# A two-layer streaming encoder in fp32r: a combined first transfer, tokens of both halves scaled together, and weight-stationary pooling and convolution projections in the second layer

## The chip, the cores and the metric

The kernel runs on one core of a Trainium2 chip. The metric is the device time of one execution in microseconds; a profiled execution gives the span of the instructions and, beside it, its own device time.

## The reference

Two layers, each with a mixing part and a feed-forward part, on 256 tokens of 1024 channels:

```
h = rmsnorm(x, g_pre_mix)
c_q, c_kv, k_r, p_in, s_u, s_v, cv_b, cv_c, cv_x, gate_logits = split(h @ w_in)
y_a = mla_branch(c_q, c_kv, k_r, ...) @ w_br_a       # attention, 8 heads, low rank q and kv, rotary part
y_b = pool_branch(p_in, pool_w, pool_scale) @ w_br_b # trailing means over 2, 4, 8, 16 tokens
y_c = sgu_branch(s_u, s_v, ...) @ w_br_c             # gating over blocks of 128 tokens
y_d = conv_branch(cv_b, cv_c, cv_x, conv_w) @ w_br_d # z = cv_c * cv_x; y = cv_b * conv3(z)
x = x + rmsnorm((sum of sigmoid(gate_i) * y_i) @ w_out, g_post_mix)
h = rmsnorm(x, g_pre_ffn)
x = x + rmsnorm((silu(h @ w_ffn_gate) * (h @ w_ffn_up)) @ w_ffn_down, g_post_ffn)
```

All arrays are fp32.

## The kernel before, in words

**Products.** TensorE multiplies in fp32r. Each fp32 operand is split into a high part (rounded to fp32r) and a remainder, and a product is three matmuls (`mac`, L316 to L320): high by high, remainder of the tokens by high weights, high tokens by remainder of the weights.

**Tokens.** The 256 tokens are two halves h of 128. The normed input is kept transposed, channels on partitions: tiles `hh` and `hl` (high and remainder) per half, eight blocks of 128 channels each. The reciprocal root of the mean square is not applied to them; it scales the results of the projections, as a column per token (`rstd`).

**Weights.** All weights lie in DRAM as 268 pieces of up to 128 x 1024 (`wall`), in the order in which they are used (`piece_plan`). Each is loaded by SP into one of four landing buffers `st` (L253), converted by ScalarE to its high part (L268), and VectorE subtracts to get the remainder (L288); both go to buffers `u4` (u in the profile), of which there are 24. `pump` does this for one piece, `tick` calls it as long as fewer than about six converted pieces are unused, and `W` hands a piece out. A buffer comes back when its last matmul has read it.

**Order.** The order on each engine is the order of the calls: the kernel turns automatic scheduling off. Side work (attention, the small branches) stands in Python generators; `tick` is called after every unit of six matmuls and advances each generator whose delay has run out. The table at the top (PA, Y1, AS and others) sets these delays in ticks.

**The start.** ScalarE issues the DMAs of the first token block and of the table of constants `cst` (L367, L370); SP issues the first two weight pieces in halves, and more tokens. Fourteen rows of matmuls on zeros (NW = 7, L387) keep TensorE busy. Then tokens are scaled by the gains, a half at a time (`x_hi`, `x_lo`), and the first two pieces converted in halves (L581, L582). The first matmuls stand in L909.

**Second layer's projections.** Groups of columns of `w_in`: A (attention), S (spatial gating), P (pooling input and cv_b), C (cv_c and cv_x), then four gates of two 512-column blocks each. For P and C (L964, L966) tokens are stationary and the weights move: `group2` runs four pieces for two halves. ScalarE evicts a half with the scale `rstd` (L932, L936), VectorE multiplies cv_c by cv_x (L937). `g_misc` then transposes the results, 12 blocks of 128 x 128 on TensorE (L789, L793), into tiles with channels on partitions, in which pooling and convolution run along the free dimension.

**Feed-forward.** Here the kernel already has blocks with stationary weights (`block`, L1092): 128 columns of the weights are stationary and the tokens move, high and remainder parts of both halves side by side as 512 columns (L1097), then the weights' remainder by the 256 high columns (L1102). The result has channels on partitions; `total` (L1106) adds the two parts and multiplies by a row of scales `rrow`, made by two transposes (`g_rrow`).

Of the kernel before, what the change touches and what calls it, by code (L numbers as in the profile page):

```python
# [10 lines left out]
F32 = mybir.dt.float32  # L11
F32R = mybir.dt.float32r
# [29 lines left out]
PA, PB = 2, 4  # L42
SA, SB = 3, 3
NW = 7
# [28 lines left out]

def down_after(b):
# [37 lines left out]
def uses(key):  # L112

    if key[1] in ("wg", "wu"):
        return 1
    return 4 if key[1] in ("uq", "ukv") or key[1] == "fd" and key[2] >= NB - 4 else 2
# [80 lines left out]
def trunk(ctx: ExitStack, tc, x, xT, wall, small, const, qtab, gpost, out):  # L197
# [64 lines left out]

    def convert(i):
        key, w = PLAN[i]
        st = staged.pop(i)
# [88 lines left out]

    def hT_tiles(h):
        return T([P, NK, P], f"hh{h}", 1, F32R), T([P, NK, P], f"hl{h}", 1, F32R)
# [3 lines left out]
    cst = T([P, 96 + NL * SGW], "cst", 1, pool=cp)  # L360
# [195 lines left out]

    def x_hi(k, eng=nc.scalar):
        for h in range(2):
            o, i, g = ht[h][0][:, k, :], xt[k // 4][:, k % 4, h * P:(h + 1) * P], sg["gpm"][:, k:k + 1]
            if eng is nc.vector:  # L560
                nc.vector.tensor_scalar(o, i, g, None, op0=ALU.mult)
            else:
                nc.scalar.activation(o, i, AF.Identity, scale=g)

    def x_lo(k):
        for h in range(2):
            nc.vector.scalar_tensor_tensor(ht[h][1][:, k, :], xt[k // 4][:, k % 4, h * P:(h + 1) * P],
                                           sg["gpm"][:, k:k + 1], ht[h][0][:, k, :].bitcast(F32),
                                           op0=ALU.mult, op1=ALU.subtract)


    first_w = {i: (U([P, PIECE], F32R), U([P, PIECE], F32R)) for i in range(2)}
    state["free"] -= 4
    src = [staged.pop(i) for i in range(2)]
    for k in range(2):
        x_hi(k, nc.vector if k == 0 else nc.scalar)
        x_lo(k)
        for i in range(2):
            w = PLAN[i][1] // 2
            c = np.s_[:, k * w:k * w + w]  # L580
            nc.scalar.activation(first_w[i][0][c], src[i][c], AF.Copy)  # L581
            nc.vector.tensor_tensor(first_w[i][1][c], src[i][c], first_w[i][0].bitcast(F32)[c], op=ALU.subtract)  # L582
    for i in range(2):
        known(i, *first_w[i])
    state["cv"] = 2
    stage_to(5)
    for kp in range(1, 4):
# [22 lines left out]
    class Part:  # L610


        def __init__(self, tiles, s, h):
            self.tiles, self.s, self.h = tiles, s, h

        def __getitem__(self, at):
            k = at[1]
            return self.tiles[k // 2][:, k % 2, self.s, self.h * P:(self.h + 1) * P]
# [611 lines left out]
```

## Time and profile before

| | |
|---|---|
| Runs (3) | median 802.87 us, 802.28 to 803.49 |
| Profiled execution | 802.21 us |
| its span | 800.4 us |
| TensorE busy | 790.8 us (99%) |
| VectorE busy | 598.3 us (75%) |
| ScalarE busy | 452.6 us (57%) |
| DMA traffic | 148.11 MB, mean 185 GB/s |

Rows of the profile name an engine (PE is TensorE, PEld its weight loads, DVE VectorE, ACT ScalarE), a line of the kernel, an operation, the tile written and the tiles read, and how often; behind the bar or after the start stand durations. An arrow in brackets says what ended the idle time before an instruction. Matmuls overlap: a duration runs from issue to the last result, so the cost of one in a row of many is the distance between starts, which the chain of waits gives.

### The profile page before, as it was taken

The numbers are of one execution on the slowest core, as the hardware profiler recorded it, in microseconds if no ns is written. First come the engines' busy times: TensorE is split into PE (matmuls) and PEld (weight loads), VectorE is DVE, ScalarE is ACT, GpSimd is POOL, SyncE is SP. The second block draws the span as 40 slices with busy tenths as digits, with TensorE's granted clock in tenths as the row PEclk, the third lists the DMA queues.
The fourth block names the chain that finished last, engine by engine and source line by source line (L and its number), as shares of the span: only waits on it lengthen the run. The fifth ranks groups of instructions, "written<-read, shape, count | busy, mean of one in ns | idle before, by whom it ended". The sixth has DMA issues, their size and how long they took to land.

```text
span 800.4 us, 10903 instructions
## 1 busy us (share of the span) xinstructions
PE 790.8 (99%) x3982; PEld 666.3 (83%) x3982; DVE 598.3 (75%) x1094; ACT 452.6 (57%) x776; POOL 3.9 (0%) x16
## 2 busy tenths in 40 slices
PE   8999999999999999999999999999999999999996
PEld 8888887888888888888888888878888888888885
DVE  6687976758887777778895688764679787777773
ACT  7767655444665555455665675644367555455541
POOL 0000000000000000000000000000000000000000
PEclk9999999999999999999999999999999999999999
DMA  9866444465664565555655545455555555555631
GB/s 317 304 215 212 160 158 158 160 208 164 201 214 136 185 205 185 186 192 176 223 170 197 205 161 182 131 172 197 175 193 184 181 185 186 187 185 185 206 106 52
DMA packets 42245, 148.11 MB, mean 185 GB/s; under 512 B 4688, under 2 KB 5840, under 8 KB 42192
## 3 DMA queue, kind: packets, MB, share of 16 engines
q1 hardware_dynamic: 41328, 145.12, 54.4%
q0 software_dynamic: 576, 2.10, 0.8%
q8 instruction: 31, 0.51, 0.3%
q10 hardware_dynamic: 288, 0.21, 0.1%
q14 instruction: 22, 0.18, 0.1%
HBM read 146.36 MB, written 1.05 MB: 184 GB/s over the span
## 4 chain that ended last, share of the span: by engine, by line
PE 98%; DVE 1%; DMA 0%; ACT 0%; issue 0%; DVEq 0%; SPq 0%; ACTq 0%
PE acc L318 20%; PE acc L320 20%; PE acc L319 20%; PE mm L1097 17%; PE mm L1102 9%; PE tp L440 3%; PE mm L318 2%; PE mm L320 2%; PE mm L319 2%; PE mm L715 1%; PE acc L743 1%; PE acc L909 1%; DMA st<-wall 0%; PE mm L836 0%; PE mm L862 0%; DVE mrg L500 0%
## 5 line engine op out<-in xcount | busy, mean ns | idle before, releaser
L288 DVE TENSOR_TENSOR u<-st,u 128x1024 fp32r<-128x1024 f32 (+1 forms) x268 | 318.6, 1214 | 50.6 <-ACT u L268 50.0
L268 ACT ACTIVATE u<-st 128x1024 fp32r<-128x1024 f32 (+1 forms) x268 | 273.5, 1047 | 17.0 <-DMA st<-wall 16.8
L318 PE MATMUL acc<-u,hh 128*128 128x512 f32 (+1 forms) x424 | 169.1, 399 | 0.0
L320 PE MATMUL acc<-u,hh 128*128 128x512 f32 (+1 forms) x424 | 164.5, 388 | 0.0
L319 PE MATMUL acc<-u,hl 128*128 128x512 f32 (+1 forms) x424 | 164.2, 387 | 0.0
L1097 PE MATMUL mm<-u,u 128*128 128x512 f32 x576 | 144.4, 392 | 0.0
L1097 PEld LDWEIGHTS mm<-u,u 128*128 128x128 f32 x576 | 105.3, 188 | 20.8
L318 PE MATMUL acc<-u,s2k 128*128 128x512 f32 x256 | 101.2, 395 | 0.0
L320 PE MATMUL acc<-u,s2k 128*128 128x512 f32 x256 | 100.6, 393 | 0.0
L319 PE MATMUL acc<-u,s2k 128*128 128x512 f32 x256 | 100.3, 392 | 0.0
L320 PEld LDWEIGHTS acc<-u,hh 128*128 128x128 f32 x424 | 79.6, 188 | 16.2
L318 PEld LDWEIGHTS acc<-u,hh 128*128 128x128 f32 x424 | 79.7, 188 | 14.5 <-issue 0.3
L319 PEld LDWEIGHTS acc<-u,hl 128*128 128x128 f32 x424 | 79.8, 188 | 14.2
L1102 PEld LDWEIGHTS mm<-u,u 128*128 128x128 f32 x576 | 78.6, 190 | 5.6
L1102 PE MATMUL mm<-u,u 128*128 128x256 f32 x576 | 80.3, 282 | 0.0
L1025 ACT ACTIVATE gate<-acc,rhalf 128x512 f32<-128x512 f32 x32 | 22.0, 689 | 65.9 <-PE acc L320 65.7
L320 PEld LDWEIGHTS acc<-u,s2k 128*128 128x128 f32 x256 | 48.1, 188 | 10.1
L318 PEld LDWEIGHTS acc<-u,s2k 128*128 128x128 f32 x256 | 48.2, 188 | 9.3 <-issue 0.3
L319 PEld LDWEIGHTS acc<-u,s2k 128*128 128x128 f32 x256 | 48.1, 188 | 9.1
L1108 DVE TENSOR_TENSOR tok<-mm,tok 128x256 f32<-128x256 f32 x72 | 30.3, 420 | 27.7 <-ACT tok L1107 27.5
L1107 ACT COPY tok<-mm 128x256 f32<-128x256 f32 x72 | 26.6, 370 | 42.6 <-PE mm L1102 39.6
L443 ACT ACTIVATE s2k<-tok 128x256 fp32r<-128x256 f32 (+1 forms) x38 | 16.3, 429 | 53.8 <-DVE tok L1122 53.8
(172 smaller groups left out, 750.1 us busy)
## 6 DMA issues: line engine op xcount, KB each, us to landing
st<-wall SPq DMA_DIRECT2D x261, 512.0 KB, 3.8
st<-wall SPq DMA_DIRECT2D x7, 416.0 KB, 4.0
gpost<-gpost POOLq DMA_DIRECT2D x4, 512.0 KB, 4.7
x<-x SPq DMA_DIRECT2D x2, 512.0 KB, 6.0
small<-small SPq DMA_DIRECT2D x2, 512.0 KB, 4.2
u<-xT SPq DMA_DIRECT2D x3, 256.0 KB, 6.2
st<-wall SPq DMA_DIRECT2D x2, 256.0 KB, 4.3
out<-x SPq DMA_DIRECT2D x2, 256.0 KB, 2.0
```

Source lines behind the costliest of these rows:

```text
L268: nc.scalar.activation(hi[:, :w], st[:, :w], AF.Copy)
L288: nc.vector.tensor_tensor(lo[:, :w], st[:, :w], hi.bitcast(F32)[:, :w], op=ALU.subtract)
L318: nc.tensor.matmul(out_, a[0][aw], w[0][ws], start=start, stop=False)
L319: nc.tensor.matmul(out_, a[1][aw], w[0][ws], start=False, stop=False)
L320: nc.tensor.matmul(out_, a[0][aw], w[1][ws], start=False, stop=stop)
L440: nc.tensor.transpose(dst[:, i * P:(i + 1) * P], s, ident)
L443: nc.scalar.activation(hi, src, AF.Copy)
L1025: nc.scalar.activation(gt[h], pgt[h], AF.Tanh, scale=rhalf[h])
L1097: nc.tensor.matmul(o, pc_[0][:, k * P:(k + 1) * P], hx[k // 2][:, k % 2].rearrange("p s t -> p (s t)"), start=(k == 0), stop=False)
L1102: nc.tensor.matmul(o[:, :SEQ], pc_[1][:, k * P:(k + 1) * P], hx[k // 2][:, k % 2, 0, :], start=False, stop=(k == NK - 1))
L1107: nc.scalar.copy(dst, o[:, SEQ:2 * SEQ])
L1108: nc.vector.tensor_tensor(dst, o[:, 0:SEQ], dst, op=ALU.add)
```

## The change

**The start.** Two arrays from the host, `head[0]` and `head[1]`, hold each one half of the first weight piece, one block of transposed tokens and constants: the gains of the first block in head[0] (680 columns), the whole table in head[1] (830 columns). SP loads them, with the other piece's halves between them; ScalarE issues no DMA, and copies the table out of the landing buffer (L633). The tokens lie in one tile `hx` (block, part, token), so that `x_hi` and `x_lo` are one operation for both halves. A third piece is loaded and converted in halves, and there are eight warm-up matmuls.

**The second layer's P and C.** Their pieces hold 128 columns each for all channels, and run through `block` with weights stationary, eight blocks in all. `g_rrow` makes the row of scales before them, `total` evicts each block into tiles with channels on partitions, and the transposes of `g_misc` are gone in this layer.

**Weights of the second layer's first gate.** The eight pieces ("gd") don't go through SP and VectorE: POOL loads the high part straight into an fp32r buffer, ScalarE writes its negative into the remainder's buffer (L286), and a second POOL DMA adds the weights onto it in place (L287).

**First layer.** The pieces of C come ahead of those of the attention, PA goes from 2 to 3 ticks there (and in the second layer), and ScalarE makes one of the two copies of the rotary key (L752).

```diff
-PA, PB = 2, 4
+PA, PB = (3, 3), 4
-NW = 7
+NW = 8
...
-        plan += [((l, "uq", i), 1024) for i in range(2)]
-        plan += [((l, "ukv", 0), 1024)]
-        plan += [((l, "C", i), wd["C"]) for i in range(4)]
+        late = [((l, "uq", i), 1024) for i in range(2)] + [((l, "ukv", 0), 1024)]
+        conv = [((l, "C", i), wd["C"]) for i in range(4)]
+        plan += conv + late if l == 0 else late + conv
...
+    if l == 1 and g in ("P", "C"):
+        c = [a + P * i for a, b in cols[g] for i in range((b - a) // P)][key[2]]
+        return kxn(inp["w_in"][l], 0, NK, [(c, c + P)])
...
+        if by_dma(i):
+            state["free"] -= 1
+            staged[i] = U([P, PIECE], F32R)
+            nc.gpsimd.dma_start(staged[i], wall[i, :, :])
+            return
...
+    def by_dma(i):
+        key = PLAN[i][0]
+        return key[0] == 1 and key[1] == "gd"
...
+        if by_dma(i):
+            hi, lo = staged.pop(i), U([P, PIECE], F32R)
+            nc.scalar.activation(lo, hi.bitcast(F32), AF.Copy, scale=-1.0)
+            nc.gpsimd.dma_start(lo, wall[i, :, :], accum_op=ALU.add)
+            known(i, hi, lo)
+            return
...
     def hT_tiles(h):
-        return T([P, NK, P], f"hh{h}", 1, F32R), T([P, NK, P], f"hl{h}", 1, F32R)
+        if h == 0:
+            hx_now[0] = T([P, NK, 2, SEQ], "hx", 1, F32R)
+        return tuple(Part([hx_now[0]], s, h) for s in range(2))
...
-    xt_load(nc.scalar, 0, 1)
-    nc.scalar.dma_start(cst, const)
-    stage_part(0, 0)
+    heads = [T([P, PIECE], "st", NST, pool=wp)]
+    nc.sync.dma_start(heads[0][:, 0:HC + HG], head[0, :, 0:HC + HG])
     stage_part(1, 0)
-    xt_load(nc.sync, 1, 2)
-    stage_part(0, 1)
+    heads.append(T([P, PIECE], "st", NST, pool=wp))
+    nc.sync.dma_start(heads[1][:, 0:HC + CW], head[1, :, 0:HC + CW])
     stage_part(1, 1)
-    state["dma"] = 2
     xt_load(nc.sync, 2, 4)
-    stage_to(4)
-    xt_load(nc.sync, 4, 6)
-    xt_load(nc.sync, 6, 8)
+    stage_part(2, 0)
+    stage_part(2, 1)
+    state["dma"] = 3
...
+    def block(key, o, both, high, mid=None):
+        pc_ = W(key)
+        for k in range(NK):
+            nc.tensor.matmul(o, pc_[0][:, k * P:(k + 1) * P], both(k), start=(k == 0), stop=False)
+            if k == 5:
+                if mid is not None:
+                    mid()
+                tick()
+        for k in range(NK):
+            nc.tensor.matmul(o[:, :SEQ], pc_[1][:, k * P:(k + 1) * P], high(k), start=False, stop=(k == NK - 1))
+        return o
+
+    def total(dst, o, tmp, rrow):
+        nc.scalar.copy(tmp, o[:, SEQ:2 * SEQ])
+        nc.vector.tensor_tensor(tmp, o[:, 0:SEQ], tmp, op=ALU.add)
+        nc.vector.tensor_tensor(dst, tmp, rrow, op=ALU.mult)
...
         else:
-            group2(l, ("P",), hT, pp, 512, evict_p)
-        pc = [acc(), acc()]
-        group2(l, ("C",), hT, pc, 512, evict_c)
+            zcp = [tok()[:, :].rearrange("p (c t) -> p c t", c=2) for _ in range(3)]
...
+            for i in range(4):
+                o = block((l, "P", i), tp() if i == 2 else mm(), both, high)
+                finish(rr)
+                evict_pc("P", i, o)
+                tick()
+            for i in range(4):
+                evict_pc("C", i, block((l, "C", i), acc(), both, high))
+                tick()
```

More of the change, by code (lines that the diff above doesn't have):

```diff
@@ L71 @@
 SGW = _o
+HA = 416
+HC = HA + SEQ
+HG = SG["gpm"][1]
+CW = 96 + NL * SGW
 def down_after(b):
@@ L196, in trunk @@
 @with_exitstack
-def trunk(ctx: ExitStack, tc, x, xT, wall, small, const, qtab, gpost, out):
+def trunk(ctx: ExitStack, tc, x, xT, wall, small, head, qtab, gpost, out):
     nc = tc.nc
@@ L577, in trunk @@
         x_lo(k)
[L578 to L583, printed above, removed]
+        split_part(0, k, heads[k][:, 0:HA])
+        split_part(1, k, src[1][:, 512 * k:512 * k + 512])
+    nc.scalar.copy(cst, heads[1][:, HC:HC + CW])
+    stage_to(4)
+    xt_load(nc.sync, 4, 6)
+    for k in range(2):
+        x_hi(2 + k)
+        x_lo(2 + k)
+        split_part(2, k, src[2][:, HA * k:HA * k + HA])
+    for i in range(3):
         known(i, *first_w[i])
-    state["cv"] = 2
+    state["cv"] = 3
     stage_to(5)
-    for kp in range(1, 4):
+    xt_load(nc.sync, 6, 8)
+    pump(1)
+    settle()
+    for kp in range(2, 4):
         for k in range(2 * kp, 2 * kp + 2):
@@ L608, in trunk, with rows_in, rows_out, g_rrow @@
     turn = None
[L610 to L618, printed above, removed]
+    def rows_in(rs):
+        rb = tok()
+        for h in range(2):
+            nc.vector.tensor_copy(rb[:, h * P:(h + 1) * P], rs[h].to_broadcast([P, P]))
+        return rb
+    def rows_out(rrow, rb):
+        t = tp()
+        transposes(t, [rb[:, h * P:(h + 1) * P] for h in range(2)])
+        nc.scalar.copy(rrow, t[:, :SEQ])
+    def g_rrow(rrow, rs):
+        rb = rows_in(rs)
+        yield RW
+        rows_out(rrow, rb)
+    def block(key, o, both, high, mid=None):
[13 more added lines that the diff above has]
+        nc.vector.tensor_tensor(dst, tmp, rrow, op=ALU.mult)
     for l in range(NL):
@@ L962, in trunk, with both, high, evict_pc @@
                 tick()
-        else:
-            group2(l, ("P",), hT, pp, 512, evict_p)
-        pc = [acc(), acc()]
-        group2(l, ("C",), hT, pc, 512, evict_c)
+            pc = [acc(), acc()]
+            group2(l, ("C",), hT, pc, 512, evict_c)
+        else:
+            zcp = [tok()[:, :].rearrange("p (c t) -> p c t", c=2) for _ in range(3)]
+            for i in (0, 2):
+                nc.gpsimd.memset(zcp[i][:, :, 0:PAD], 0.0)
+            row = row1
+            htile = hx_now[0]
+            def both(k):
+                return htile[:, k].rearrange("p s t -> p (s t)")
+            def high(k):
+                return htile[:, k, 0, :]
+            def evict_pc(g, i, o):
+                dst = zcp[(2 if i < 2 else 1) if g == "P" else 0][:, i % 2, PAD:PAD + SEQ]
+                v = tok()
+                if g == "C" and i >= 2:
+                    total(v[:, 0:SEQ], o, v[:, 0:SEQ], row)
+                    nc.vector.tensor_tensor(dst, dst, v[:, 0:SEQ], op=ALU.mult)
+                else:
+                    total(dst, o, v[:, 0:SEQ], row)
+            for i in range(4):
[6 more added lines that the diff above has]
+                tick()
         sm = small_load(l)
@@ L1113, in gate_up @@
             gv, uv = v[:, 0:SEQ], v[:, SEQ:2 * SEQ]
-            o = block(("wg", b))
+            o = block((l, "wg", b), mm(), both, high)
             if b == B0:
                 finish(rr)
-            total(gv, o)
+            total(gv, o, gv, rrow)
             nc.scalar.activation(sg_[:, :SEQ], gv, AF.Sigmoid)
@@ L1120, in gate_up @@
             tick()
-            total(uv, block(("wu", b)))
+            total(uv, block((l, "wu", b), mm(), both, high), uv, rrow)
             nc.vector.tensor_tensor(gv, gv, uv, op=ALU.mult)
@@ L1140, in down, with both, high @@
                         start=(b == 0), stop=(b == NB - 1))
+        def both(k):
+            return hx[k // 2][:, k % 2].rearrange("p s t -> p (s t)")
+        def high(k):
+            return hx[k // 2][:, k % 2, 0, :]
         gact = [None, None]
@@ L1200, in build @@
     with tile.TileContext(nc) as tc:
-        trunk(tc, ap["x"], ap["xT"], ap["wall"], ap["small"], ap["const"], ap["qtab"], ap["gpost"], out)
+        trunk(tc, ap["x"], ap["xT"], ap["wall"], ap["small"], ap["head"], ap["qtab"], ap["gpost"], out)
     return nc
@@ L1211, in host_arrays @@
     const, qtab = host_const(inp)
+    xT = np.ascontiguousarray(x.T.reshape(NK, P, SEQ).transpose(1, 0, 2))
+    head = np.zeros((2, P, HC + CW), np.float32)
+    for k in range(2):
+        head[k, :, 0:HA] = wall[0, :, k * HA:(k + 1) * HA]
+        head[k, :, HA:HC] = xT[:, k, :]
+    head[0, :, HC:HC + HG] = const[:, 96:96 + HG]
+    head[1, :, HC:] = const
     return {
         "x": x,
-        "xT": np.ascontiguousarray(x.T.reshape(NK, P, SEQ).transpose(1, 0, 2)),
+        "xT": xT,
         "wall": wall,
         "small": np.stack([host_small(inp, l) for l in range(NL)]),
-        "const": const,
+        "head": head,
         "qtab": qtab,
```

126 lines of the change are left out of this document (63 added, 63 removed).

## The prediction

> **What bounds the kernel now.** I read the page's totals and its chain of waits first, then the busy time by stretches, then the start and the second layer's projections instruction by instruction.
>
> ```profile
> span 800.4 us, 10903 instructions
> PE 790.8 (99%) x3982; PEld 666.3 (83%) x3982; DVE 598.3 (75%) x1094; ACT 452.6 (57%) x776; POOL 3.9 (0%) x16
> PE 98%; DVE 1%; DMA 0%; ACT 0%; issue 0%; DVEq 0%; SPq 0%; ACTq 0%
> ```
>
> TensorE is the bound over the whole span: 98% of the chain that ended last is its own work. So time can come only from the start, from the tail (untouched here), from matmuls that go away, or from a new wait of TensorE.
>
> ```profile
> 5.60:7.40 1.80, 1.73 (x5) 1.69 (x6) 1.80 (x6) 1.24 (x3) 0.00 (x0) 1.00 1.01 320
> 7.40:9.20 1.80, 1.80 (x6) 1.48 (x6) 1.80 (x6) 1.45 (x4) 0.00 (x0) 1.00 1.01 407
> 9.20:12.50 3.30, 3.30 (x17) 2.89 (x16) 2.53 (x6) 3.00 (x7) 0.00 (x0) 1.00 1.04 400
> 20.00:40.00 20.00, 20.00 (x92) 16.94 (x91) 12.62 (x22) 15.11 (x22) 0.00 (x0) 1.00 0.89 303
> ```
>
> These rows give, after the stretch, TensorE's busy time and matmuls, then weight loads, VectorE, ScalarE, POOL, clock, DMA share and GB/s. From 5.6 to 9.2 us TensorE does 11 matmuls in 3.6 us though it is busy all the time; after that it does 17 in 3.3. The first ones run at about half speed, whatever the clock column says: 3.6 us for work that would take 2.1 at the later rate (11 x 3.3 / 17), or 1.8 at exactly half; a loss of 1.5 to 1.8 us. From 20 us on there is no gap.
>
> ```profile
> 1.05 3.36 PE L387 MATMUL mm<-tok 128*128 128x128 f32 x14 [1.05 <-DVE warm L383]
> 3.50 0.55 ACT L581 ACTIVATE u<-st 128x416 fp32r<-128x416 f32 x1 [0.34 <-DMA st<-wall]
> 4.95 0.63 ACT L581 ACTIVATE u<-st 128x512 fp32r<-128x512 f32 x1 [0.90 <-DMA st<-wall]
> 5.24 0.48 DVE L561 TENSOR_SCALAR hh<-u,cst 128x128 fp32r<-128x128 f32 x2 [4.23 <-DMA cst<-const]
> 5.67 1.03 PE L909 MATMUL acc<-u,hh 128*128 128x416 f32 x2 [1.26 <-ACT u L581]
> 10.74 1.06 ACT L268 ACTIVATE u<-st 128x1024 fp32r<-128x1024 f32 x1 [0.30 <-DMA st<-wall]
> 11.84 1.22 DVE L288 TENSOR_TENSOR u<-st,u 128x1024 fp32r<-128x1024 f32 x1 [0.33 <-ACT u L268]
> 15.17 0.40 PE L320 MATMUL acc<-u,hh 128*128 128x512 f32 x1
> ```
>
> The first real matmul waits until 5.67, and the last thing to land for it is the table of constants (VectorE starts at 5.24 after waiting for cst).
>
> **The change, part 1: the start.** ScalarE's queue opens like this in the kernel before (u is a weight or token buffer, st a landing buffer, cst the constants, hh the scaled tokens of one half).
>
> ```order
> L367 DMA u_8_76<-xT 128x256
> L370 DMA cst_70<-const 128x158
> L388 ACT_TABLE_LOAD
> L388 ACTIVATE warm_71<-warm_71 128x1
> L581 ACTIVATE u_18_112<-st_80 128x416
> L581 ACTIVATE u_20_114<-st_82 128x512
> L563 ACTIVATE hh_4_72<-u_8_76,cst_70 128x128
> L563 ACTIVATE hh_6_74<-u_8_76,cst_70 128x128
> ```
>
> Two DMAs come first there, and tokens take one operation a half. After the change it opens so (hx holds both parts and both halves of the tokens; st_75 and st_79 are the two head transfers):
>
> ```order
> L429 ACT_TABLE_LOAD
> L429 ACTIVATE warm_71<-warm_71 128x1
> L621 ACTIVATE u_16_106<-st_75 128x416
> L621 ACTIVATE u_18_108<-st_77 128x512
> L611 ACTIVATE hx_72<-st_79 128x256
> L621 ACTIVATE u_16_106<-st_79 128x416
> L621 ACTIVATE u_18_108<-st_77 128x512
> L633 COPY cst_70<-st_79 128x158
> ```
>
> Both DMAs leave ScalarE's queue for SP's, where the first transfer (680 columns, 340 KB) carries weights, tokens and gains. The first landings bracket it: 208 KB at 3.50, and at 4.95 all of the first 592 KB (208 + 128 + 256). In proportion, 340 KB are there at about 4.0. VectorE scales 256 columns (0.35 to 0.48), ScalarE converts 416 weights (0.55): ready at 4.6. An eighth warm-up (the 14 rows of 3.36 us are seven) ends about then, so TensorE runs on without its idle gap: start 5.67 to 4.6, **1.05 us** gained.
>
> With no gap, the half speed should also end sooner. Up to 1.8 us are to be had, but the next cap is near: the fourth weight piece has 2451 KB landed ahead of and with it, against 2447 KB before, so it still lands at 10.7, is converted by 11.8 and its remainder is subtracted by 13.05 (rows at 10.74 and 11.84). The matmul that needs this remainder ran at 15.17; it cannot run before 13.1. So the start is worth between 1.05 (half speed lasts as long as before) and 2.1 us (the cap). I take **1.9**. VectorE does one operation for two halves there, which only adds slack.
>
> The Trainium skill, TensorE: Matmul & The Clock Gate, Part 1, says that the array runs at half clock until one whole window of about 3.4 us, which runs freely and isn't reset, has been busy. The half speed in the rows above agrees, as warm-ups with a gap behind them did not end it. By that rule, with work from 1.05 us on without a gap, full speed would come between about 4.5 and 7.9 us, an estimate of 1.8 us gained on average.
>
> **Part 2: pooling and convolution projections.** TensorE in the kernel before, inside the second layer's pooling group (hh0/hl0: both parts of the first half's tokens):
>
> ```order
> L318 MATMUL acc_841_4112<-u4_821_4001,hh0_784_3828 128x512
> L319 MATMUL acc_841_4112<-u4_821_4001,hl0_785_3829 128x512
> L320 MATMUL acc_841_4112<-u4_822_4002,hh0_784_3828 128x512
> L318 MATMUL acc_841_4112<-u4_831_4043,hh0_784_3828 128x512
> L319 MATMUL acc_841_4112<-u4_831_4043,hl0_785_3829 128x512
> ```
>
> Tokens are stationary, one half at a time. After, with the row of scales (tok_824) transposed first and the weights stationary:
>
> ```order
> L481 MATMUL tp_836_4095<-ident_1_69,tok_824_4021 128x128 x2
> L691 MATMUL mm_840_4104<-hx_780_3810,u4_805_3928 128x512 x8
> L697 MATMUL mm_840_4104<-hx_780_3810,u4_806_3929 128x256 x8
> L691 MATMUL mm_845_4131<-hx_780_3810,u4_810_3955 128x512 x8
> L697 MATMUL mm_845_4131<-hx_780_3810,u4_811_3956 128x256 x8
> ```
>
> 96 matmuls of 512 columns become 64 of 512 and 64 of 256; 12 transposes go, 2 come. The feed-forward part already runs such blocks:
>
> ```profile
> 237.93 1.85 PE mm L1097 x8
> 239.79 0.95 PE mm L1102 x8
> 405.67 0.23 PE acc L319
> 395.16 0.44 PE tp L440 x4
> ```
>
> Eight blocks cost 8 x (1.85 + 0.95) = 22.4 us; before, 96 x 0.23 = 22.1 (a matmul of 512 columns takes 1.85 / 8 to 0.23). Transposes at 0.44 / 4 = 0.11: minus 10 x 0.11 = 1.1. Net **minus 0.7 us**; minus 1.1 if the narrow matmuls cost nothing extra, minus 0.3 if the transposes were half hidden.
>
> **Part 3: the gate pieces, where a wait can appear.** Each block is evicted by a ScalarE copy and two VectorE operations, eight times, and VectorE is relieved of eight subtractions of 1.2 us: the weights of the first gate branch come through POOL, and their remainder is a ScalarE pass (L286) followed by an accumulating DMA. ScalarE's queue before the gates, in the kernel before (u4_811 and u4_807: attention inputs; u4_886: second remainder):
>
> ```order
> L268 ACTIVATE u4_873_4230<-st_846_4132 128x1024
> L268 ACTIVATE u4_876_4245<-st_849_4156 128x1024
> L658 ACTIVATE u4_811_3955<-u4_811_3955,ry_870_4223 128x256
> L659 ACTIVATE u4_811_3955<-u4_811_3955,ry_870_4223 128x128
> L658 ACTIVATE u4_811_3955<-u4_811_3955,ry_870_4223 128x256
> L659 ACTIVATE u4_811_3955<-u4_811_3955,ry_870_4223 128x128
> L268 ACTIVATE u4_881_4285<-st_853_4170 128x1024
> ```
>
> Here the scalings have only conversions ahead. In the changed kernel the same place reads:
>
> ```order
> L286 ACTIVATE u4_880_4284<-u4_851_4165 128x1024
> L702 COPY tok_881_4297<-acc_878_4272 128x256
> L744 ACTIVATE u4_807_3937<-u4_807_3937,ry_872_4244 128x256
> L745 ACTIVATE u4_807_3937<-u4_807_3937,ry_872_4244 128x128
> L744 ACTIVATE u4_807_3937<-u4_807_3937,ry_872_4244 128x256
> L745 ACTIVATE u4_807_3937<-u4_807_3937,ry_872_4244 128x128
> L286 ACTIVATE u4_886_4323<-u4_856_4192 128x1024
> ```
>
> Before, the loads' conversions (L268) stood there and VectorE finished them. The second remainder now stands behind the four scalings, which wait for VectorE's reciprocal root, and a DMA follows it.
>
> ```profile
> 432.34 0.29 DVE L632 TENSOR_TENSOR tok<-u,cst 128x32 f32<-128x32 f32 x2
> 433.74 0.25 DVE L650 COPY kr<-kr 128x96 f32<-128x96 f32 x1
> 434.98 0.17 DVE L410 TENSOR_SCALAR ry<-rv 128x4 int32<-128x4 int32 x1
> 439.12 0.51 ACT L658 ACTIVATE u<-u,ry 128x256 f32<-128x256 f32 x1 [2.47 <-DVE ry L419]
> 440.52 1.05 ACT L268 ACTIVATE u<-st 128x1024 fp32r<-128x1024 f32 x1
> 443.87 0.37 ACT L447 ACTIVATE s2k<-tp,cst 128x128 fp32r<-128x128 f32 x1 [0.74 <-DVE s2k L448]
> 444.65 0.37 ACT L447 ACTIVATE s2k<-tp,cst 128x128 fp32r<-128x128 f32 x1 [0.42 <-DVE s2k L448]
> L1107 ACT COPY tok<-mm 128x256 f32<-128x256 f32 x72 | 26.6, 370 | 42.6 <-PE mm L1102 39.6
> L1108 DVE TENSOR_TENSOR tok<-mm,tok 128x256 f32<-128x256 f32 x72 | 30.3, 420 | 27.7 <-ACT tok L1107 27.5
> 448.91 0.53 POOL L489 DMA_DIRECT2D gpost<-gpost  x1 [0.22 <-DVE rhalf L974]
> DMA to landing us min/median/max: 3.8/4.7/4.9
> ```
>
> Count from the first pooling block, at 0. The fourth ends at 11.2, its copy at 11.75. VectorE then has, in order: three evictions of 2 x 0.42, the rotary work 1.65 (432.34 to 433.99), two subtractions of 1.22, twelve small root steps of 0.2: 9.0 us, about 0.3 less as neighbours overlap, so 20.5. Four scalings 1.4 (439.12 to 440.52): 21.9. The pass 1.05: 22.9. POOL issues, and the data are there L later. TensorE has eight blocks (22.4), eight transposes (0.9), and eight gate matmuls (1.8) ahead of the matmul that reads them: 25.0 (25.1 by these figures; some matmuls overlap). It is late by L - 2.1. The fourth remainder then stands behind another pass, two copies and six alternating scalings (0.8 a pair, rows 443.87 and 444.65): issued at 30.5, wanted at 32.0 plus the first delay; it adds 0.6. Together L - 1.5.
>
> No trace here has an accumulating DMA. The nearest is POOL's other 512 KB transfer: 3.8 to 4.9 us from issue to landing. An accumulate reads its destination too, so twice 3.8 is the upper bound; the lower is nothing at all, if VectorE runs 2 us ahead of my count. I take L = 4.0: **plus 2.5 us** (0 to 6.1).
>
> The Trainium skill, DMA: Bandwidth & Descriptors, Anatomy of one DMA, fits POOL-issued DMAs at 2.0 us plus the bytes over 436 GB/s; for 512 KB an estimate of 3.2 us, and by it this term would be 1.7.
>
> **Hidden edits.** In the first layer convolution weights move ahead of the attention's; every queue there has slack (20 to 40 us shows TensorE without a gap), and the one copy moved from VectorE to ScalarE is 1.2 us on an engine with 4.9 us idle in those 20. Without that cover each would cost up to its own length. Eight loads leave SP's queue, so what stands behind them there is issued earlier, and become 16 on POOL's; their high parts are issued some 20 us before use. POOL's memset (0.3) and gpost now stand behind the third remainder, but are needed only after the gates. On ScalarE, the evictions of the last two convolution blocks are queued behind the passes; their readers come later than the gates. The table copy at the start (0.3 us) delays one token scaling that TensorE needs 2 us later.
>
> **The sum.** The profiled execution took 802.21 us, the median of the runs is 802.87. 802.21 - 1.9 - 0.7 + 2.5 = **802.1**. A measurement of this kernel can tell about 0.2%, 1.6 us, from no change: 801.3 to 804.5 is the same.
>
> **Rivals.**
> - The remainders arrive in time (VectorE is ahead of my count, or the transfer is short): 802.21 - 2.6 + 0.4 = 800.0. For it: VectorE has 25% of the span free. Against: it is loaded just there. Chance 0.30.
> - The accumulating transfer is slow: at L = 7.6 the second gate remainder is 5.5 late, 6.1 in all, 805.7. It decides for slower from L = 6.4, where the term is 4.9. For it: reading and writing one buffer; two other transfers on the queue. Chance 0.17.
> - The half speed stays: the warm-ups do not count, as 3.36 us of them did not help before. 802.21 - 1.05 - 0.7 + 2.5 = 803.0. By the clock rule named above this needs a gap in the work. Chance 0.13.
> - My forecast: 0.40, of which a quarter (the term under 1.7) lies below 801.3.
>
> Faster 0.30 + 0.10 = 0.40; slower 0.17 and a little of the third, 0.18; same 0.42. The range goes from 799.7 (nearly all hidden) to 805.0 (L near 7).
>
> **What would show it.** First L999 matmul at 4.6, full speed by 8; eight blocks of 2.8 us with no idle between; TensorE idle at L345 of the first gate, released by POOL's DMA, 1 to 3 us. No idle there and a time near 800 refute part 3; a first matmul after 5 us refutes part 1.

## The result, and the profile after

The changed kernel takes **813.03 us** (median of 4 runs, 812.59 to 814.55) where the kernel before takes 802.78: ratio 1.0129, interval 1.0114 to 1.0144. It is 10.2 us slower. The prediction's sum went from 802.21, the profiled execution, to 802.1, with a range of 799.7 to 805.0; the measured time lies far outside. The profiled execution took 812.59. Its totals and its chain of waits:

```profile
span 810.8 us, 10976 instructions
PE 792.3 (98%) x4006; PEld 665.4 (82%) x4006; DVE 594.5 (73%) x1095; ACT 451.3 (56%) x771; POOL 15.4 (2%) x32
PE 86%; DMA 5%; DVE 3%; issue 3%; ACT 2%; POOL 1%; SPq 0%; DVEq 0%; POOLq 0%; ACTq 0%
```

TensorE's work is nearly the same (792.3 against 790.8), but it is no longer the whole chain: 86% in place of 98%. To see where the time went, the transposes of x ahead of the two feed-forward parts serve as marks. First the kernel before, then the changed one (TensorE's rows on x, 195 to 420 us and 590 to 640; the last two times are the first and the last start):

```profile
L440 PE MATMUL tp<-ident,x x32: 270/272/327, 208.0 to 407.0; 128*128 128x128 f32 x32
L440 PE MATMUL tp<-ident,x x16: 270/272/273, 601.9 to 615.9; 128*128 128x128 f32 x16
```

```profile
L481 PE MATMUL tp<-ident,x x32: 270/272/329, 212.5 to 411.5; 128*128 128x128 f32 x32
L481 PE MATMUL tp<-ident,x x16: 270/272/273, 612.5 to 626.5; 128*128 128x128 f32 x16
```

Up to the first feed-forward part 4.5 us are lost (208.0 to 212.5), from there to the second one 6.1 more (393.9 to 400.0). The feed-forward parts themselves last the same: 187.0 us from the first mark to the second layer's first transposes of x, and 190.9 from the second mark to TensorE's last matmul, in both. In the tables below, "first" is the first mark, "second" the distance to the other one.

The start came as forecast. The stretches of the start, as in the prediction, and TensorE's first rows behind the warm-ups:

```profile
1.05:4.49 3.44, 3.44 (x17) 3.44 (x17) 0.86 (x3) 1.72 (x3) 0.26 (x1) 1.00 0.73 220
5.60:7.40 1.80, 1.80 (x10) 1.52 (x9) 0.75 (x2) 0.64 (x2) 0.00 (x0) 1.00 1.01 298
```

```profile
4.49 6.08 PE L999 MATMUL acc<-u,hx 128*128 128x416 f32 x24
10.41 0.35 PE L343 MATMUL acc<-u,hx 128*128 128x416 f32 x1
```

The warm-ups run up to the first real matmul without a gap, that one starts at 4.49 (forecast 4.6), and from 5.6 us on 10 matmuls take 1.8 us, where the kernel before needed 3.6 us for 11: full speed comes some 3.6 us sooner. The group's first L343 starts at 10.41; the same matmul started at 12.43 before. So 2.0 us are won there (forecast 1.9).

Part of that belongs to these two executions and not to the change. Seven traces of this study have the old start. In five of them, the kernel before among them, the half speed lasts until 9.2 to 10.6 us. In the other two (e10 and f3 of the experiments below) matmuls run at full speed from the first ones at about 5.7 us on, in spite of the gap before them. This is the second of the two stretches in f3, where the kernel before does 6 matmuls:

```profile
7.40:9.20 1.80, 1.80 (x10) 1.53 (x9) 1.80 (x6) 1.78 (x6) 0.00 (x0) 1.00 0.98 394
```

In the twelve traces with the new start, full speed comes at 4.4 us in the earliest and at 7.1 in the latest. The matmul that starts at 10.41 here starts at 10.1 to 11.4 us in them, and at 11.1 to 12.9 us with the old start: 1.7 us apart in the mean.

What was won is lost again. If the same matmuls are compared, 1.1 of the 2.0 us are left between 22 and 44 us (times of the kernel before). Then the changed kernel falls behind, by 2.1 us at 58, 2.8 at 69 and 4.5 at 87 us. TensorE's waits between 40 and 62 us, and between 440 and 475 (in all, times, longest):

```profile
PE acc L345 <- DVE u L313: 1.3, 1, 1.3
PE tp L481 <- DVE s2k L489: 0.8, 1, 0.8
PE acc L343 <- ACT u L293: 0.4, 1, 0.4
PE tp L481 <- ACT u L744: 0.3, 1, 0.3
```

```profile
PE acc L345 <- DMA u<-wall: 6.2, 3, 3.0
```

In the kernel before, TensorE waits for nothing in either stretch. The second list is the wait that part 3 of the prediction spoke of, with 6.2 us where 2.5 were forecast; the first list was not forecast at all.

### The profile page after: what moved, and what is told of

It is laid out like the page before. It is cut to its first block, busy times and chain, and to the rows that moved or that the text cites. A ratio compares the mean times of both kernels' runs of the same rounds, so it can differ in the third digit from the quotient of the medians.

```text
span 810.8 us, 10976 instructions
## 1 busy us (share of the span) xinstructions
PE 792.3 (98%) x4006; PEld 665.4 (82%) x4006; DVE 594.5 (73%) x1095; ACT 451.3 (56%) x771; POOL 15.4 (2%) x32
## 3 DMA queue, kind: packets, MB, share of 16 engines
HBM read 150.56 MB, written 1.05 MB: 187 GB/s over the span
## 4 chain that ended last, share of the span: by engine, by line
PE 86%; DMA 5%; DVE 3%; issue 3%; ACT 2%; POOL 1%; SPq 0%; DVEq 0%; POOLq 0%; ACTq 0%
PE acc L345 17%; PE acc L343 17%; PE acc L344 17%; PE mm L691 17%; PE mm L697 9%; DMA st<-wall 3%; PE tp L481 2%; DVE u L313 2%; PE mm L345 1%; PE mm L343 1%; PE mm L344 1%; DMA u<-wall 1%; PE mm L802 1%; PE acc L830 1%; ACT u L293 1%
## 5 line engine op out<-in xcount | busy, mean ns | idle before, releaser
L313 DVE TENSOR_TENSOR u<-st,u 128x1024 fp32r<-128x1024 f32 (+1 forms) x259 | 308.1, 1215 | 43.8 <-ACT u L293 43.7
L293 ACT ACTIVATE u<-st 128x1024 fp32r<-128x1024 f32 (+1 forms) x259 | 264.1, 1047 | 16.4 <-DMA st<-wall 14.4
L345 PE MATMUL acc<-u,hx 128*128 128x512 f32 (+1 forms) x392 | 152.6, 389 | 8.0 <-DMA u<-wall 6.2
L343 PE MATMUL acc<-u,hx 128*128 128x512 f32 (+1 forms) x392 | 156.6, 399 | 0.4 <-ACT u L293 0.4
L344 PE MATMUL acc<-u,hx 128*128 128x512 f32 (+1 forms) x392 | 151.8, 387 | 0.0
L343 PE MATMUL acc<-u,s2k 128*128 128x512 f32 x256 | 101.0, 394 | 0.0
L345 PEld LDWEIGHTS acc<-u,hx 128*128 128x128 f32 x392 | 73.6, 188 | 25.2 <-DMA u<-wall 7.5
L343 PEld LDWEIGHTS acc<-u,hx 128*128 128x128 f32 x392 | 73.8, 188 | 14.0 <-issue 0.7
L344 PEld LDWEIGHTS acc<-u,hx 128*128 128x128 f32 x392 | 73.8, 188 | 12.9
L1145 ACT ACTIVATE gate<-acc,rhalf 128x512 f32<-128x512 f32 x32 | 22.1, 690 | 66.2 <-PE acc L345 66.1
L343 PEld LDWEIGHTS acc<-u,s2k 128*128 128x128 f32 x256 | 48.2, 188 | 9.1
```

The lines of the kernel that those rows point to most:

```text
L293: nc.scalar.activation(hi[:, :w], st[:, :w], AF.Copy)
L313: nc.vector.tensor_tensor(lo[:, :w], st[:, :w], hi.bitcast(F32)[:, :w], op=ALU.subtract)
L343: nc.tensor.matmul(out_, a[0][aw], w[0][ws], start=start, stop=False)
L344: nc.tensor.matmul(out_, a[1][aw], w[0][ws], start=False, stop=False)
L345: nc.tensor.matmul(out_, a[0][aw], w[1][ws], start=False, stop=stop)
L1145: nc.scalar.activation(gt[h], pgt[h], AF.Tanh, scale=rhalf[h])
```

## The experiments

Ratios are against the kernel before on the same chip. Marks are in us, from the profiled execution, which need not be near the median (it took 803.55 us for e4, 807.76 for e7 and 803.78 for e12).

| run | median us | ratio (interval) | first | second |
|---|---|---|---|---|
| before | 802.78 | 1 | 208.0 | 393.9 |
| changed | 813.03 | 1.0129 (1.0114 to 1.0144) | 212.5 | 400.0 |
| e1_old_start | 813.23 | 1.0131 (1.0117 to 1.0144) | 212.4 | 400.0 |
| e2_old_layer0 | 809.66 | 1.0088 (1.0074 to 1.0102) | 209.0 | 400.1 |
| e3_gates_by_sp | 808.12 | 1.0069 (1.0055 to 1.0083) | 212.8 | 396.0 |
| e4_e2_and_e3 | 804.38 | 1.0026 (1.0016 to 1.0036) | 207.9 | 395.9 |
| e5_mult_on_pool | 806.03 | 1.0043 (1.0030 to 1.0055) | 209.2 | 397.1 |
| e6_conv_first | 804.82 | 1.0025 (1.0016 to 1.0035) | 209.6 | 396.0 |
| e7_pa_3 | 806.71 | 1.0048 (1.0035 to 1.0062) | 211.8 | 396.3 |
| e8_copy_on_act | 805.49 | 1.0034 (1.0021 to 1.0046) | 209.1 | 396.0 |
| e9_pa_2 | 809.74 | 1.0088 (1.0075 to 1.0101) | 209.9 | 400.1 |
| e10_blocks_only | 806.93 | 1.0057 (1.0043 to 1.0070) | 208.4 | 398.2 |
| e11_start_only | 803.20 | 1.0004 (0.9995 to 1.0013) | 209.2 | 394.1 |
| e12_start_own | 802.18 | 0.9993 (0.9985 to 1.0002) | 209.9 | 394.1 |
| f1_sum_in_psum | 803.01 | 1.0002 (0.9994 to 1.0011) | 208.3 | 393.6 |
| f4_no_mult | 802.43 | 1.0000 (0.9991 to 1.0009) | 209.5 | 393.7 |
| f2_gates_by_dma_only | 807.71 | 1.0074 (1.0061 to 1.0087) | 208.4 | 398.3 |
| f3_half_by_dma | 803.54 | 1.0013 (1.0004 to 1.0022) | 209.4 | 394.9 |
| f5_start_and_sum | 802.11 | 0.9989 (0.9980 to 0.9999) | 209.8 | 393.7 |

The second distance repeats within 0.4 us in runs whose second layer is alike (395.9 to 396.3 in e3, e4, e6, e7 and e8). The first does not: e2, e4 and e5 have the same first layer and 209.0, 207.9 and 209.2. Differences of about 1 us there are read from whole times, with care. As the runs are spread over several chips, on which the kernel before took 802.48 to 802.85, what an edit costs is taken from the ratios; a difference of two of them is known to about 1.5 us.

### Which half of the change: the start, the first layer, the gates

```diff
 e1   -  SP loads head[0], head[1]          + ScalarE loads tokens and cst, NW = 7, as before
 e2   -  plan += conv + late if l == 0 else late + conv
      +  plan += late + conv
      -  PA, PB = (3, 3), 4                 + PA, PB = (2, 3), 4
      -  copy = nc.scalar.copy if e and l == 0 else nc.vector.tensor_copy
      +  copy = nc.vector.tensor_copy
 e3   -  return key[0] == 1 and key[1] == "gd"
      +  return False
 e4      e2 and e3
```

> The changed kernel with the start of the kernel before (two transfers on ScalarE's queue, seven warm-ups, two pieces in halves); all else as changed. Theory A: the new start causes the first layer's stalls (TensorE idle 5.6 us between 44 and 88 us), because its two head transfers occupy landing buffers, SP issues nothing between 5.8 and 8.5 us, the weight stream falls to 157 GB/s at 12 us, and ScalarE and VectorE then run 1.6 us later against a slack of 0.5 us. By it the first layer comes back to the time of the kernel before and the whole to about 808.5. Theory B: the stalls come from the first layer's reordered pieces, the longer delay PA and the rotary copy on ScalarE. By it the stalls stay (a little shorter, as TensorE starts 1.1 us later), the gain at the start is lost, and the time is 812 to 815.

> The changed kernel with the first layer's order of pieces, its PA and its rotary copy as before; the new start and all of the second layer as changed. Theory A (the new start causes the stalls): idle time between 44 and 88 us stays at 3 us or more, the whole at 810 or over. Theory B (order, PA and copy cause them): they go, and the whole comes to about 807.5 (813.0 - 5.5). In both the second layer's stalls stay at 6 to 7 us.

> The changed kernel with the second layer's first gate weights loaded by SP and split by ScalarE and VectorE as all others. Theory C: the three stalls at the first gate (3.19 + 1.67 + 1.83 = 6.7 us) are the accumulating DMAs, which landed 5.2 to 12.4 us after issue and stood behind each other on POOL's queue. By it the stalls go and the time is about 806.3 (813.0 - 6.7). Rival D: without them VectorE has eight more subtractions of 1.22 us in the same stretch, beside the evictions of the eight blocks, and the gates wait for VectorE instead: 3 us or more of idle stays at the first gate, and the time is 809 or over.

> Both of the edits before in one kernel: what is left of the change is the new start and the weight-stationary blocks of the second layer. If theory B and C hold and the parts are independent: 813.0 - 5.5 - 6.7 = 800.8, faster than the kernel before by 2.0 (1.3 from the start, 0.8 from the transposes). If theory A holds: 804 to 806. If rival D holds: 803 to 805 as well, but with the idle time at the first gate.

Undoing the start changes nothing (813.23), although TensorE then starts 1.4 us later: behind a later stall an earlier start is worth nothing, and the stalls are not its work. Theory A falls. B holds in the main: the first layer's three small edits are worth 3.3 us (809.66), where B had 5.5. The gates' DMA is worth 4.8 (808.12, where theory C had 6.7), both together 8.3. But e4 is still slower than the kernel before, where it was expected to be faster. Its second part has lost 2.0 us without any accumulating DMA: rival D, at least in part. In e3 and e4 TensorE waits at the first gate for VectorE's remainders instead (1.3 us).

### The three small edits of the first layer

```diff
 e6   e4 with    + plan += conv + late if l == 0 else late + conv
 e7   e4 with    + PA, PB = (3, 3), 4
 e8   e4 with    + copy = nc.scalar.copy if e and l == 0 else nc.vector.tensor_copy
```

> The run of both edits with the first layer's pieces of C ahead of the attention's again; PA and the rotary copy stay as before. Theory B1: the order alone makes the first layer's stalls (idle between 44 and 60 us): the first layer ends 3 to 4.5 us later, 807.5 to 809 in all. If it is one of the other two edits, nothing changes: 804.4.

> The run of both edits with PA at 3 ticks in the first layer again. Theory B2: the later start of the attention's splits makes the stalls: 807 or over. Else 804.4, or a little less, as the splits then come after the gates' first remainders.

> The run of both edits with one of the two rotary copies of the first layer on ScalarE again. Theory B3: this copy (1.0 us) stands ahead of the conversion of the gates' second piece, which has about 0.5 us of slack, so TensorE waits there 0.5 us for the high part and 1.4 us for the remainder: 806 to 807.5. Else 804.4.

PA is the edit that costs: 1.0048 against 1.0026, or 1.8 us. The order of the pieces is not told apart from nothing. The copy on ScalarE adds 0.6 us by the ratios, less than the runs of the same first layer scatter. How a tick costs time is seen on VectorE. In e4 (PA 2), then in e7 (PA 3):

```profile
50.27 1.22 DVE L313 TENSOR_TENSOR u<-st,u 128x1024 fp32r<-128x1024 f32 x1
51.40 0.34 DVE L489 SCALAR_TENSOR_TENSOR s2k<-tp,cst,s2k 128x128 fp32r<-128x128 f32 x1
53.23 1.22 DVE L313 TENSOR_TENSOR u<-st,u 128x1024 fp32r<-128x1024 f32 x1
```

```profile
52.01 2.35 DVE L313 TENSOR_TENSOR u<-st,u 128x1024 fp32r<-128x1024 f32 x2
54.67 0.34 DVE L489 SCALAR_TENSOR_TENSOR s2k<-tp,cst,s2k 128x128 fp32r<-128x128 f32 x1
56.64 0.44 PE L481 MATMUL tp<-ident,tok 128*128 128x128 f32 x2 [0.79 <-DVE s2k L489]
```

With PA 2 the attention's splits (L489) begin behind one remainder of the gates; with PA 3 behind two and an eviction, 3.3 us later, and TensorE's next transposes wait for them, as they use the same PSUM tile. Between 50 and 69 us e7 falls back by 1.4 us. A second loss, of 1.7 us, follows between 77 and 87 us in every trace with PA 3 in the first layer (changed, e1, e3, e7) and in none with PA 2. There the pooling branch's matmul waits for VectorE; here in e7 (80 to 90 us):

```profile
PE mm L926 <- DVE tok L921: 0.5, 1, 0.5
```

How the tick delays that branch was not followed. How thin the cover was is in the trace of before. There the second gate piece's remainder and the matmul that reads it stand so:

```profile
50.24 1.22 DVE L288 TENSOR_TENSOR u<-st,u 128x1024 fp32r<-128x1024 f32 x1
51.98 0.39 PE L320 MATMUL acc<-u,hh 128*128 128x512 f32 x1
```

It is ready at 51.46 and read at 51.98: half a microsecond of slack in a stretch without any gap.

### PA in the change, and the blocks alone

```diff
 e9   changed kernel with      - PA, PB = (3, 3), 4     + PA, PB = (2, 2), 4
 e10  kernel before with the weight-stationary blocks of the second layer (PA 2 in both)
```

> The changed kernel with PA back at 2 ticks in both layers, and nothing else. Theory E: PA is the larger part of the first layer's loss (alone it cost 2.3 us there) and part of the second layer's, since the attention's splits then stand behind the gates' first conversions and evictions: about 809 or under (813.0 - 2.5 or more in the first layer, - 1 or more in the second). Rival: in the full change the order of the pieces and the copy on ScalarE keep the stalls, 811 to 813.

> The kernel before with the weight-stationary pooling and convolution blocks of the second layer alone (start, first layer, gate loads and PA as before). Theory E: the second layer's 2.1 us of loss without the DMA gates come from PA; then the blocks alone give the 0.3 to 0.8 us of the transposes: 802.0 to 802.5. Theory D (VectorE's evictions in the attention's chain cost it): 804 to 805.

In the full change too PA is the first layer's larger loss: 809.74, 3.3 us less; in the profiled executions the first mark comes 2.6 us earlier. In the second layer theory E falls: there the blocks lose 4.3 us with PA 2 (398.2) and 2.0 with PA 3 (395.9 in e4); the longer delay helps. With the DMA gates the second part is 400.0 to 400.1 with either. The blocks alone are 0.57% slower than no change.

### Why the blocks cost time

```diff
 e5   e4 with      total(..., eng=nc.gpsimd):   eng.tensor_tensor(dst, tmp, rrow, op=ALU.mult)
 f4   blocks alone, PA (2, 3):   - nc.vector.tensor_tensor(dst, tmp, rrow, op=ALU.mult)
 f1   blocks alone, PA (2, 3):
-     nc.tensor.matmul(o, w, both(k), ...)
+     for s in range(2):
+         nc.tensor.matmul(o[:, :SEQ], w, parts[:, k, s, :], ...)
-     total(dst, o, tmp, row)
+     nc.vector.tensor_tensor(dst, o[:, 0:SEQ], row, op=ALU.mult)
```

> The run of both edits (old first layer, gates by SP) with one more: the multiplication by the row of scales, eight operations of 0.43 us in the second layer's eight blocks, goes from VectorE to POOL. Theory D: the blocks cost the second layer 2.1 us because their evictions (16 operations of 0.42 us) stand in VectorE's queue ahead of the attention's chain and of the gate pieces' remainders. With 3.4 us fewer on VectorE the three idle times at the first gate (0.95, 0.70, 0.71 us) go, and the time falls from 804.4 to about 802. Rival: POOL needs longer than VectorE for each, or slows VectorE, so that the pooling inputs or the queue are no earlier: 804 or over.

> The kernel before with the weight-stationary blocks alone, PA (2, 3), and the multiplication by the row of scales left out of the eight evictions (pooling and convolution inputs then are not scaled): 3.4 us less on VectorE, nothing else changed. Theory D: the idle time at the first gate (0.95 + 0.70 + 0.70 us) goes or falls under 0.7, and the time is about 802.5 to 803. Rival F: it stays, 804.5.

> The kernel before with the weight-stationary blocks alone, PA (2, 3), and the two parts of a block summed in PSUM: three matmuls of 256 columns a channel block in place of one of 512 and one of 256, so that the eviction is one VectorE operation and no ScalarE copy. It adds 8 x (24 x 0.119 - 1.85 - 0.95) = 0.5 us of matmuls and takes 3.4 us off VectorE and 3.0 off ScalarE. Theory D (the evictions in VectorE's queue make the 2.1 us): the second layer loses 0.5 or less, 802.5 to 803.5 in all. Rival F: the loss comes from the order of blocks, attention and gates (the gates' first pieces come sooner, as the blocks need each piece once), and stays: 804.5 or over.

Busy times from 433 to 450 us (TensorE, weight loads, VectorE, ScalarE, POOL) in the kernel before, in e4 and in f4 (there from 434.6 to 451.6, as it reaches the second layer 1.6 us later), each of the two with TensorE's waits from 440 to 475 us behind it:

```profile
433.00:450.00 17.00, 17.00 (x83) 14.01 (x82) 13.23 (x35) 11.27 (x26) 1.02 (x4) 1.00 0.54 186
```

```profile
433.00:450.00 17.00, 16.22 (x91) 13.71 (x90) 15.40 (x43) 9.24 (x24) 0.00 (x0) 1.00 0.48 155
```

```profile
PE acc L345 <- DVE u L313: 1.3, 2, 0.8
PE mm L343 <- DVE u L773: 0.5, 1, 0.5
```

```profile
434.60:451.60 17.00, 17.00 (x95) 14.69 (x94) 15.11 (x42) 10.04 (x26) 0.00 (x0) 1.00 0.52 181
```

```profile
PE mm L343 <- DVE u L759: 0.4, 1, 0.4
```

The blocks turn ScalarE's evictions into VectorE's. In e4 VectorE goes up by 2.2 us in 17, and TensorE waits for its remainders. f4 leaves out the multiplications, so pooling and convolution get unscaled inputs. In it the waits for remainders are gone, and the second part takes 393.7. VectorE is hardly less busy in this stretch (15.11 against 15.40 us). But the remainder that TensorE waited for first starts earlier, by 1.8 us counted from the start of the layer. In e4, then in f4:

```profile
446.01 1.22 DVE L313 TENSOR_TENSOR u<-st,u 128x1024 fp32r<-128x1024 f32 x1
```

```profile
445.84 1.22 DVE L313 TENSOR_TENSOR u<-st,u 128x1024 fp32r<-128x1024 f32 x1
```

So the order of the blocks (rival F) costs nothing; VectorE's evictions ahead of the remainders do. f1 does with one eviction operation a block and keeps the result: three narrow matmuls sum in PSUM, TensorE waits for nothing there, and the second part is the shortest of all (393.64). That is 0.2 us under the kernel before (393.85): this is what the blocks have to give. f1 and f4 have PA 3 in the second layer and the kernel before has 2; what that tick does alone in the second layer was not run.

e5 fails, by its rival. Its rows on VectorE and POOL:

```profile
435.24 0.61 DVE L724 TENSOR_TENSOR kr<-tok 128x16 f32<-128x16 f32 x1
435.77 0.16 DVE L725 TENSOR_TENSOR kr<-tok 128x16 f32<-128x16 f32 x1
```

```profile
435.08 0.74 POOL L704 TENSOR_TENSOR tok<-tok,rrow 128x256 f32<-128x256 f32 x1 [1.14 <-DVE tok L703]
```

POOL takes 0.74 us here (1.08 on average) for what VectorE does in 0.43, and a VectorE operation beside it takes 0.61 in place of 0.17. TensorE's waits for remainders grow to 2.1 us.

### The accumulating transfers by themselves

```diff
 f2   kernel before with      by_dma(i):  key[0] == 1 and key[1] == "gd"
 f3   kernel before with      by_dma(i):  key[0] == 1 and key[1] == "gd" and key[2] == 1
```

> The kernel before with the eight pieces of the first gate loaded by POOL (cast and accumulate) alone; projections, start, first layer and PA as before. Theory C: the accumulating transfers land 5 us or more after issue and stand behind each other on POOL's queue, so the gate waits even with VectorE unloaded: 3 to 5 us, 806 to 808. Rival: only together with the blocks, which delay ScalarE's scalings and so the second pass, is the transfer late; alone it fits, and VectorE is relieved: 802 to 803.

> As the run before, but only the four pieces of the gate's second column block go by POOL. Theory C: they have some 10 us more until they are used, and only four accumulating and four casting transfers share the queue, each landing in 5 to 7 us: no idle time at the gates, 802.7, and VectorE's relief buys nothing, as it did not end a wait there. Rival: two passes and two queues cost ScalarE its order, 804 or over.

They are late by themselves: f2 loses 4.4 us in the second part, without any block, 3.1 of them at the gates by the distance between starts. Landing times of the accumulating DMAs, in the changed kernel, in f2 and in f3 (the loads by SP: 3.6 us on the changed kernel's page), f2 and f3 with TensorE's waits at the gates behind it:

```profile
DMA to landing us min/median/max: 5.2/7.9/12.4
```

```profile
DMA to landing us min/median/max: 5.5/7.8/9.7
```

```profile
PE acc L345 <- DMA u<-wall: 2.8, 2, 1.9
```

```profile
DMA to landing us min/median/max: 7.2/7.8/8.1
```

```profile
PE mm L908 <- DVE tok L903: 0.7, 1, 0.7
```

With half as many, and later used ones, no matmul of the gates waits for a DMA any more. But nothing is gained either: the second part is 1.0 us longer than before, as a wait for VectorE appears later (in the pooling branch's matmul). The chain of orders behind that wait was not followed. Nor do they land any sooner: f3's four are issued 2.7 to 4.3 us apart, and the one ahead of the first of them on POOL's queue lands 0.3 us after its issue. Still they take 7.2 to 8.1 us. So waiting behind each other is not the whole reason; the rest stays open.

### The start by itself, and a version from the parts

```diff
 e11  kernel before with the new start
 e12  e11 with
-     heads = [T([P, PIECE], "st", NST, pool=wp)]
+     heads = [U([P, PIECE])]
      (and pieces 3 and 4 and the tokens issued directly behind)
 f5   e12 and f1 in one kernel
```

> The kernel before with the new start alone (one SP transfer for weights, tokens and gains, tokens of both halves in one operation, third piece in halves, eight warm-ups). As I forecast in the prediction, it would give 1.9 us: 800.9. Theory A2: the 2.0 us that it is ahead at the second group are lost again before 40 us, since two head transfers take landing buffers and the weight stream has a hole at 11 to 13 us: the first layer ends between 0.1 us earlier and 1.2 later than in the kernel before, 802.5 to 804.

> The run before with one more: the two head transfers land in two of the 24 weight buffers, which are free then, so that the four landing buffers hold pieces 1 to 4, and SP issues pieces 3 and 4 and the tokens without waiting for the head to be read. Theory A2: the hole in the weight stream at 11 to 13 us closes, and part of the 2.0 us is kept: 801 to 802. Rival: the start is bound by the bytes, as the stream runs at 350 to 400 GB/s either way, and nothing is kept: as the run before.

> The two parts that lost nothing in one kernel: the new start with its head transfers in weight buffers (0.9993 of the kernel before, by itself not clear) and the blocks summed in PSUM (1.0002; the second layer 0.2 us shorter in its trace). If both are independent: 802.0, a ratio of 0.999. Rival: the first layer is bound by its weight stream up to 40 us, so that the start gives nothing, and the time is that of the kernel before.

Alone, the start gives nothing (1.0004). The rows at 11 to 13 us, kernel before, then changed, then e11 (last column GB/s):

```profile
11.00:13.00 2.00, 2.00 (x12) 1.72 (x11) 1.67 (x3) 1.97 (x5) 0.00 (x0) 1.00 1.04 399
```

```profile
11.00:13.00 2.00, 2.00 (x12) 1.85 (x10) 1.17 (x2) 1.79 (x4) 0.00 (x0) 1.00 0.80 178
```

```profile
11.00:13.00 2.00, 2.00 (x12) 1.98 (x11) 1.34 (x3) 1.88 (x4) 0.00 (x0) 1.00 0.90 271
```

The head transfers hold landing buffers, and the weight stream sinks to 178 GB/s, in e11 to 271. (That SP issues nothing between 5.8 and 8.5 us is no difference: the kernel before pauses from 6.1 to 8.4.) e12 keeps the buffers free and issues the next loads at once. In its trace the stream is at 404 and 420 GB/s there, its median is 1.0 us under e11, and its interval still holds no change.

This hole is not where e11 loses its lead. Here the same matmuls are compared with those of the kernel before (us; plus is ahead):

| start in the kernel before | 12.4 | 32.9 | 38.3 | 43.7 | 50.1 |
|---|---|---|---|---|---|
| e11 | +1.4 | +1.5 | +1.0 | -0.6 | -1.2 |
| e12 | +1.7 | +1.1 | +0.7 | -1.2 | -1.9 |
| f3 (old start) | +1.2 | +1.2 | +1.2 | -0.7 | -1.4 |

All three fall back between 33 and 50 us, f3 without the new start; an earlier start does not last, wherever it comes from. In e11 the conversion of one and the same piece stands so, and then in the kernel before:

```profile
36.15 1.06 ACT L293 ACTIVATE u<-st 128x1024 fp32r<-128x1024 f32 x1 [2.03 <-DMA st<-wall]
```

```profile
34.74 1.06 ACT L268 ACTIVATE u<-st 128x1024 fp32r<-128x1024 f32 x1 [0.56 <-DMA st<-wall]
```

The piece lands 1.4 us later, though TensorE is ahead. TensorE's waits from 3 to 45 us in e12, and in the kernel before:

```profile
PE acc L345 <- DVE u L313: 1.1, 2, 0.5
PE acc L343 <- ACT u L293: 0.3, 1, 0.3
PE acc L1001 <- ACT u L626: 0.2, 1, 0.2
```

```profile
PE acc L909 <- ACT u L581: 1.3, 1, 1.3
```

The kernel before waits once, at the start; e12 starts early and waits at 37 to 41 us, for pieces that have just landed. The wait moves, it doesn't go. Why these pieces land late, in e12 without the hole at 11 to 13 us, stays open. Together with f1 it makes the kernel with the lowest ratio, f5: 0.9989, interval 0.9980 to 0.9999, which is 0.9 us and under what I called measurable.

## Why the prediction was wrong, point by point

- **What bounds the kernel**: right, TensorE. The conclusion from it was wrong: I took a stretch without a gap on TensorE for slack on the other queues. The slack was 0.5 us.
- **Start, minus 1.9**: the mechanism was right in each step (4.49 for 4.6, no gap, full speed before 8 us, 2.0 us won at 10.4). Agreement with the Trainium skill, TensorE: Matmul & The Clock Gate, Part 1 (half clock until a window of about 3.4 us was busy): from 1.05 us on without a gap, full speed came at 5.6, inside the span worked out from it (4.5 to 7.9), and at 4.4 to 7.1 in all traces with this start. In e10 and f3, though, 3.36 us of warm-ups with a gap behind them were enough, so half speed behind the gap is no rule, and the 1.5 to 1.8 us that I read off one trace are not lost each time. The failing step is the cap: I looked for it at one piece, the fourth, which did land at 10.74 as I said. The pieces that are read at 37 to 45 us came late, and e11's lead of 1.5 us was gone by 44 us. Measured: 0 (e11), and 0.6 with free buffers, in an interval that holds 0 (e12).
- **Blocks, minus 0.7** (0.8 by its own rows, 22.4 - 22.1 - 1.1): measured without the eviction work minus 0.2 (f4, and f1 with its narrow matmuls), beside the end of minus 0.3 that I gave. But their evictions cost 2.0 us with PA 3 and 4.3 with PA 2 when the gates come by SP (e4, e10, f4). In the sum I had set them only into the count of the gate's second remainder, where the removed subtractions offset them.
- **Gates, plus 2.5 (0 to 6.1)**: the place and the count were right, and so was the wait as such; the size was not. ScalarE's second pass, POOL's issues and the matmul that waits:

```profile
447.29 1.04 ACT L286 ACTIVATE u<-u 128x1024 fp32r<-128x1024 f32 x1
448.64 0.88 POOL L287 DMA_DIRECT2D u<-wall  x1 [5.27 <-ACT tok L702]
449.85 1.12 POOL L287 DMA_DIRECT2D u<-wall  x1
450.74 0.40 PE L344 MATMUL acc<-u,hx 128*128 128x512 f32 x1
454.16 0.51 PE L345 MATMUL acc<-u,hx 128*128 128x512 f32 x1 [3.02 <-DMA u<-wall]
```

  The first block starts at 425.79. The pass is done 22.5 us later (forecast 22.9), the data are wanted at 25.2 (25.0). L was 5.5 in place of 4.0, so the first wait is 3.2, close to L - 2.1. That is luck in part: the eight landed after 5.2 to 12.4 us, and this one was the second shortest. The failing step is "the fourth adds 0.6" and nothing for the third: these two remainders landed 8.8 and 10.2 us after issue. From 448 to 471 us the transfers of POOL's queue, casting loads among them, landed in the order of issue, one every 1.1 to 3.5 us. TensorE lost 1.7 and 1.8 us more, 6.7 in all by the distance between starts. The second rival named this queue, with a chance of 0.17. The estimate of 3.2 us for 512 KB, from the fit in the Trainium skill (DMA: Bandwidth & Descriptors, Anatomy of one DMA), does not hold for these transfers: the lowest for an accumulating one was 5.2.
- **Hidden edits, 0**: the largest miss of a single term. PA alone costs 1.8 us (e7), undone in the full change 3.3 (e9), and all three edits cost 3.3 (e2). PA stood among the edits, and I gave it no term.

The parts as measured, by the ratios: first layer's edits 3.3, gates 4.8, blocks and start 2.1 (e4), 10.2 together. Nearly all of the last is the blocks, as the start alone gives nothing.

## What to carry to other kernels

A bound engine without a gap says nothing of how close the queues behind it are. Before an edit beside it is costed at nothing, look up how long ahead of its reader each result stands, and cost the edit against that. An operation moved to a queue that holds the conversions is paid when those are the next to be waited for, whatever the engine's mean load is. And a transfer that others are queued with is costed by the spacing of the queue and by landing times of its own kind, not by one landing time of another kind. Last, a gain at the start is worth something only if what TensorE reads later comes sooner too.

## What the runs showed of the hardware

- POOL-issued accumulating transfers of 512 KB landed after 5.2 us at best and 7.8 to 7.9 in the median, even with 2.7 us or more between issues (f3); 3.6 for loads by SP.
- A POOL multiplication of 128 x 256 fp32 took 0.74 to 1.08 us against 0.43 on VectorE, and lengthened a small VectorE operation beside it from 0.17 to 0.61.
- After the same 3.36 us of warm-up matmuls and the same gap, five traces ran the first real matmuls at half speed until 9.2 to 10.6 us and two at full speed from about 5.7 us; the clock column read 1.00 in both cases.
- Executions with the same first layer differ by up to 1.3 us at the first mark (207.9 to 209.2), while the second part repeats within 0.4 us.
